# Moving the powers of C and the Toeplitz taps of a state-space group behind the chain of its states

## The chip, the cores and the metric

The kernel runs on one core of one Trainium2 chip. The metric is the device time of one execution in microseconds, as the median of several runs. The core has five engines that each work through a queue of their own in order: PE (TensorE, matrix products; its weight loads are shown as PEld), DVE (VectorE), ACT (ScalarE), POOL (GpSimd) and SP (SyncE, which here only issues DMAs). An instruction that waits holds up everything behind it in its queue.

## What is computed

One layer of a hybrid decoder, for a prompt of 1024 tokens and for 8 sequences of 4 new tokens each, D_MODEL 1024. The normed input is multiplied with one matrix whose 3072 columns are `x_ssm | z_ssm | q | k | v | z_attn`, 512 each. One branch is a state-space layer (S5), the other a dilated sliding-window attention; both are normed, joined and projected out. The change is in the state-space branch:

```python
bu_re = jnp.einsum('btgc,gpc->btgp', u, Bb_re)      # 32 groups of 16 channels, 64 complex states each
...
_, _, x_re, x_im = lax.associative_scan(_complex_affine_combine, (a_re, a_im, bu_re, bu_im), axis=1)
y = (jnp.einsum('btgp,gcp->btgc', x_re, C_re.astype(f32))
     - jnp.einsum('btgp,gcp->btgc', x_im, C_im.astype(f32))
     + D.astype(f32).reshape(N_SSM_GROUPS, SSM_GROUP) * u)
```

Each group has a diagonal complex transition `lam`; its states are driven by 16 input channels through B and read out through C.

## The kernel before

**The stage around the change.** The input projection is cut into 12 blocks of 256 columns. For each block two loads bring the weights (`load_w`, L220, on SP), eight pairs of instructions split them into a high and a low part (ACT L142 and DVE L143, `split`; both operands of L143 lie in SBUF), and PE multiplies them with the normed input, three passes each (L314 for blocks whose output is transposed, L294 for the blocks of v). ACT and DVE evict the results (L335 to L344, L378, L379), and SP stores them. Blocks 8 and 0 come first. From the seven following blocks (1, 9, 5, 2, 3, 7, 4) each is interleaved with a step of the state-space layer, which takes its 32 groups in eight sets of GO = 4, called groups below: `ssm(o)` prepares set o, `outputs(o)` reads it out.

```python
    outs = [ssm(0)]
    for o, blk in enumerate(SSM_BLOCKS):
        outs.append(ssm(o + 1))
        if o == len(SSM_BLOCKS) - 1:
            outs[o]()
        in_proj(blk)
        if o < len(SSM_BLOCKS) - 1:
            outs[o]()
    outs[-1]()
```

**What `ssm(o)` does.** Time is cut into chunks of L = 8 steps. SP loads the inputs of the set, `chunk` (L580), which blocks 0 and 1 have stored to `d_u`. Then, in the text's order:

- *B's powers*: POOL multiplies tables into `wa` and `wb` (L594, L595), DVE adds them (L596), PE turns them (L600), ACT copies them to `wt` (L601).
- *C's powers and the taps*: POOL multiplies into `f2` and `f2b` (L606, L607), DVE adds them (L608). POOL makes the diagonal of D (`di`, L611). PE multiplies B with C's powers (L615), ACT copies the result to `tap` (L618, four copies), POOL adds `di` (L619), and eight DMAs on SP (L622) lay the taps out as a Toeplitz matrix in `tpl`. `tpl` is used in turn, one of two.
- *the phases*: POOL multiplies tables into `rc`, `q0`, `rs`, `q1` (L634, L635, L637, L638), DVE combines them (L636, L639).
- *the chain of the states*: PE multiplies the inputs with `wt` (L648), DVE turns the result by the phases (L650 to L656), runs the scan over the chunks (L659), POOL turns it back into `xx` (L663 to L665) and DVE adds the halves (L666); ACT copies the last state and the start states (L667, L669).

`outputs(o)` then multiplies C's powers with the states (L678) and the Toeplitz matrix with the inputs (L679) on PE, adding both in one bank; ACT applies GELU (L681) and SP stores `yo` to `d_y` (L682).

**Buffers.** `wa`, `wb`, `f2b`, `q0`, `q1` and `tap` share four buffers (tag `gen`); `u` has three; `rc`, `rs`, `f2`, `xx` and `wt` have two each. PE's banks for L615 and for L648 are the same pair (tag `ss`).

**What sets the order.** In this stage no order is written out. The framework (`schedule_with_timeline_sim=True`, L1817) lays the instructions of each engine in a queue by a timeline of its own: where several are ready, the one that stands first in the text goes first; the buffers of a tag are handed out in the text's order too. So the text's order is a priority. Behind the stage (L740 on) the steps follow a plan that the kernel works out itself.

## Time and profile before

| | us |
|---|---|
| median of 3 runs | 705.58 (705.45 to 707.25) |
| the profiled execution | 704.87 |
| its span | 703.1 |
| PE busy in the span | 650.1 |
| DVE, ACT, POOL busy | 486.1, 318.3, 294.1 |
| mean granted clock of TensorE | 0.962 of full speed |

The times of instructions come from one profiled execution. Starts count from the start of its span. A line L143 is line 143 of the kernel before; the line is that of the call inside a helper where a helper records the instruction. A row such as `2.54 <-DVE f L608` means that the engine sat idle for 2.54 us before the instruction and that L608 on DVE ended that.

### The profile page before, as it was taken

The page shows a single profiled execution, that of the slowest core. Times are in us where ns is not written, and L with a number is a line of the kernel's source. Part 1 is how long each engine was busy: PE and PEld are TensorE (multiplying, and loading weights), DVE is VectorE, ACT ScalarE, POOL GpSimd, SP SyncE. Part 2 cuts the span into 40 slices and gives each one's busy share as a digit, 9 for nine tenths or more (in the row PEclk, how much of TensorE's full clock was granted, in tenths as well). Part 3 has the DMA queues.
Part 4 walks back from the last instruction along what each step waited for, and adds up shares of the span by engine and source line. Part 5 has one row for each costly group of instructions (what it writes and reads, how often), then busy time and mean ns, then how long its engine had stood idle before and what let it go on. Part 6 is the DMA issues. An engine that isn't in the chain of part 4 may idle for free.

```text
span 703.1 us, 12224 instructions
## 1 busy us (share of the span) xinstructions
PE 650.1 (92%) x4122; PEld 594.0 (84%) x4122; DVE 486.1 (69%) x1147; ACT 318.3 (45%) x745; POOL 294.1 (42%) x292
## 2 busy tenths in 40 slices
PE   7999896999999999959898989899999799999995
PEld 5999885999989999959888979778566599887995
DVE  4997969457797672334865787488667788965386
ACT  6762251043144252343432333277466578852363
POOL 2425687545674452004767630044233345520032
PEclk9999999899999999979999889999999799999999
DMA  8713313243432553588767744598999534028023
GB/s 278 232 32 131 116 46 112 70 153 108 125 119 71 169 173 112 209 262 235 241 200 230 235 130 152 155 285 280 309 271 296 186 110 146 18 76 281 12 98 150
DMA packets 79055, 116.22 MB, mean 165 GB/s; under 512 B 15856, under 2 KB 45424, under 8 KB 78992
## 3 DMA queue, kind: packets, MB, share of 16 engines
q1 hardware_dynamic: 78992, 115.44, 52.4%
q8 instruction: 33, 0.54, 0.3%
q14 instruction: 30, 0.25, 0.1%
HBM read 83.60 MB, written 30.62 MB: 162 GB/s over the span
## 4 chain that ended last, share of the span: by engine, by line
PE 53%; DVE 17%; DMA 12%; POOL 7%; issue 4%; ACT 4%; SPq 2%; DVEq 0%; POOLq 0%; ACTq 0%
PE mm L314 13%; PE fo L1632 5%; PE ops L1537 4%; PE mm L294 4%; DMA ct<-in_cache_v_dram 4%; PE mm L1023 4%; PE ss L294 3%; PE tp L294 3%; PE ss L1480 3%; PE tp L1522 3%; POOL dm L978 3%; DMA ct<-in_cache_k_dram 3%; DVE win L143 3%; DVE pm L1483 1%; PE fo L1348 1%
## 5 line engine op out<-in xcount | busy, mean ns | idle before, releaser
L314 PE MATMUL mm<-xT,win 128*128 128x352 f32 x1008 | 172.9, 328 | 3.7 <-DVE eq L379 1.3
L314 PEld LDWEIGHTS mm<-xT,win 128*128 128x128 f32 x1008 | 163.0, 190 | 5.1 <-DVE eq L379 1.6
L1023 PE MATMUL mm<-xT,win 128*128 128x352 f32 x432 | 78.9, 338 | 2.8 <-DVE win L1005 2.8
L1503 POOL TENSOR_SCALAR pm<-pm,rd 128x128 f32<-128x128 f32 (+3 forms) x64 | 48.5, 760 | 72.3 <-DVE rd L1499 56.9
L1023 PEld LDWEIGHTS mm<-xT,win 128*128 128x128 f32 x432 | 72.5, 197 | 3.6 <-DVE win L1005 3.4
L978 POOL TENSOR_TENSOR dm<-ct,dq 128x512 f32<-128x512 f32 x40 | 51.6, 1314 | 53.0 <-DMA ct<-in_cache_k_dram 34.1
L1495 ACT ACTIVATE pm<-pm,mn 128x128 f32<-128x128 f32 (+3 forms) x64 | 49.5, 773 | 20.2 <-DVE mn L1483 17.9
L294 PE MATMUL mm<-win,xT 128*128 128x256 f32 x384 | 53.5, 294 | 1.7 <-DVE win L143 1.5
L143 DVE SCALAR_TENSOR_TENSOR win<-wst,gin,win 128x256 fp32r<-128x256 f32 x72 | 50.0, 742 | 5.5 <-ACT win L142 5.4
L1529 DVE TENSOR_TENSOR pl<-tp,ph 128x512 fp32r<-128x512 f32 (+1 forms) x80 | 50.2, 633 | 5.1 <-ACT ph L1526 4.8
L1526 ACT ACTIVATE ph<-tp 128x512 fp32r<-128x512 f32 (+1 forms) x80 | 43.1, 547 | 22.4 <-PE tp L1522 16.4
L1632 PE MATMUL fo<-wo,gh 128*128 128x512 f32 x192 | 51.8, 412 | 0.0
L294 PEld LDWEIGHTS mm<-win,xT 128*128 128x128 f32 x384 | 49.2, 197 | 2.6 <-DVE win L143 2.1
L810 PE MATMUL gl<-yh,wg 128*128 128x272 f32 (+1 forms) x256 | 51.1, 298 | 0.0
L1483 DVE CUSTOM_DVE_ANT_0 pm<-ss,maskp 128x512 f32<-128x512 f32 (+2 forms) x64 | 37.1, 582 | 16.5 <-PE ss L1480 16.1
L1522 PE MATMUL tp<-ident,pm 128*128 128x128 f32 x288 | 45.8, 278 | 0.0
L810 PEld LDWEIGHTS gl<-yh,wg 128*128 128x128 f32 x256 | 42.5, 200 | 0.0
L1632 PEld LDWEIGHTS fo<-wo,gh 128*128 128x128 f32 x192 | 35.5, 194 | 6.9 <-DVE mn L1483 0.2
L1522 PEld LDWEIGHTS tp<-ident,pm 128*128 128x128 f32 x288 | 34.7, 142 | 7.3 <-issue 2.1
L1480 PE MATMUL ss<-ka,qt 128*128 128x512 f32 (+2 forms) x96 | 36.8, 385 | 2.3 <-DMA ka<-d_k 2.3
L981 DVE TENSOR_REDUCE scd<-dm 128x8 f32<-128x512 f32 x40 | 27.1, 682 | 17.2 <-POOL dm L978 16.9
L810 PE MATMUL gl<-yl,wg 128*128 128x272 f32 (+1 forms) x128 | 37.6, 294 | 0.0
(391 smaller groups left out, 1369.6 us busy)
## 6 DMA issues: line engine op xcount, KB each, us to landing
wst<-in_w_in_dram SPq DMA_DIRECT2D x24, 512.0 KB
ct<-in_cache_k_dram SPq DMA_DIRECT2D x48, 256.0 KB
ct<-in_cache_v_dram SPq DMA_DIRECT2D x48, 256.0 KB
xt<-in_x_prompt_dram SPq DMA_DIRECT2D x8, 512.0 KB
wst<-in_w_out_dram SPq DMA_DIRECT2D x8, 512.0 KB
xres<-in_x_prompt_dram SPq DMA_DIRECT2D x8, 512.0 KB
qt<-d_q SPq DMA_DIRECT2D x32, 128.0 KB
qw<-d_q SPq DMA_DIRECT2D x32, 128.0 KB
```

What stands on the lines that cost most here:

```text
L143: V.scalar_tensor_tensor(lo, src, scale, f(hi), op0=OP.mult, op1=OP.subtract)
L294: T.matmul(out, lhs(a, kt), w(b, kt)[:, c0:c0 + cn], start=(n == 0), stop=(n == 3 * ktn - 1))
L314: T.matmul(p, w(b, kt)[:, c * 128:c * 128 + 128], x(a, kt), start=(n == 0), stop=(n == 23))
L810: T.matmul(p, wg[:, b, kt, c:c + 128], o.y[a][:, kt, :, :o.w], start=(n == 0), stop=(n == 11))
L978: GP.tensor_tensor(out=y.m, in0=y.c, in1=x.q, op=OP.mult)
L1023: T.matmul(x.p, o.w[kt][:, b, c * 128:c * 128 + 128], xT[a][:, kt, 352 * k:352 * k + 352], start=(kt == 0 and j == 0), stop=(kt == 7 and j ...
L1480: T.matmul(x.p[c][:, :w], q[:, i % 4 * 128:i % 4 * 128 + 128], o.ka[:, 512 * c:512 * c + w], start=(m == 0), stop=(m == 1))
L1495: S.activation(x.pm[:, :n], x.pm[:, :n], AF.Exp, scale=-1.0, bias=x.mn[:, nch - 1:nch], accum_out=x.dn)
L1503: a = op(PO, 0.02 + n * 0.0012, lambda: GP.tensor_scalar(x.pm[:, :n], x.pm[:, :n], x.rd, 1.0, op0=OP.mult, op1=OP.mult), pr, [a], give=["rd"])
L1522: T.transpose(x.p[:, n * 128:n * 128 + 128], o.rows[2 * m + u].pm[:, j * 128:j * 128 + 128], ident)
L1529: V.tensor_tensor(out=x.l[:, :w], in0=x.p[:, :w], in1=f(x.h[:, :w]), op=OP.subtract)
L1632: T.matmul(o.f[hf], o.g[u][:, i, k], wo[0][:, j, 2 * u + k, hf * 512:hf * 512 + 512], start=(u + k + n == 0), stop=(u + k + n == 4))
```

## The change

The block that makes C's powers, the taps and their Toeplitz layout is moved inside `ssm(o)`: it stood between the transposed powers of B and the phases, and stands now at the end, behind the last instruction of the chain of the states. No instruction is added, taken away or changed in shape. PE's L615 now comes behind L648 in the text, POOL's L606, L607, L611 and L619 behind L663 to L668, and SP's eight L622 are the last DMAs of `ssm(o)`.

```diff
--- before.py
+++ after.py
@@ -601,27 +601,6 @@
         S.activation(wt, p, AF.Copy)
 
 
-        sh9 = [128, GO, 9, CH]
-        f2, f2b = wk(sh9, "f2"), wk(sh9, "f2b")
-        GP.tensor_tensor(out=f2, in0=pw(pr, 0, 9), in1=bc(cst, 9), op=OP.mult)
-        GP.tensor_tensor(out=f2b, in0=pw(pi, 0, 9), in1=bc(csw, 9), op=OP.mult)
-        V.tensor_tensor(out=f2, in0=f2, in1=f2b, op=OP.add)
-
-        di = wk([16, GO, 16], "di")
-        GP.tensor_tensor(out=di, in0=ident[:16, :16].unsqueeze(1).to_broadcast([16, GO, 16]),
-                         in1=dd[:, gs].unsqueeze(2).to_broadcast([16, GO, 16]), op=OP.mult)
-        p = ss_ps([128, 128])
-        for g in range(GO):
-            T.matmul(p[32 * g:32 * g + 16], bb[:, g0 + g, :], f2[:, g, 0:8, :].rearrange("p t c -> p (t c)"), start=True, stop=True)
-        tap = wk([16, GO, 128], "tap")
-        for g in range(GO):
-            S.activation(tap[:, g], p[32 * g:32 * g + 16], AF.Copy)
-        GP.tensor_tensor(out=tap[:, :, 0:16], in0=tap[:, :, 0:16], in1=di, op=OP.add)
-        tpl = tpls[o % 2]
-        for s in range(8):
-            SY.dma_start(tpl[s::8, :, 16 * s:], tap[:, :, 0:128 - 16 * s])
-
-
         shr = [128, GO, 8, 16]
         rc, rs_, q0, q1 = wk(shr, "rc"), wk(shr, "rs"), wk(shr, "q0"), wk(shr, "q1")
 
@@ -668,6 +647,27 @@
         GP.memset(xx[:, :, 0:1], 0.0)
         S.activation(xx[:, :, NC:], x0[:, gs, :], AF.Copy)
 
+
+        sh9 = [128, GO, 9, CH]
+        f2, f2b = wk(sh9, "f2"), wk(sh9, "f2b")
+        GP.tensor_tensor(out=f2, in0=pw(pr, 0, 9), in1=bc(cst, 9), op=OP.mult)
+        GP.tensor_tensor(out=f2b, in0=pw(pi, 0, 9), in1=bc(csw, 9), op=OP.mult)
+        V.tensor_tensor(out=f2, in0=f2, in1=f2b, op=OP.add)
+
+        di = wk([16, GO, 16], "di")
+        GP.tensor_tensor(out=di, in0=ident[:16, :16].unsqueeze(1).to_broadcast([16, GO, 16]),
+                         in1=dd[:, gs].unsqueeze(2).to_broadcast([16, GO, 16]), op=OP.mult)
+        p = ss_ps([128, 128])
+        for g in range(GO):
+            T.matmul(p[32 * g:32 * g + 16], bb[:, g0 + g, :], f2[:, g, 0:8, :].rearrange("p t c -> p (t c)"), start=True, stop=True)
+        tap = wk([16, GO, 128], "tap")
+        for g in range(GO):
+            S.activation(tap[:, g], p[32 * g:32 * g + 16], AF.Copy)
+        GP.tensor_tensor(out=tap[:, :, 0:16], in0=tap[:, :, 0:16], in1=di, op=OP.add)
+        tpl = tpls[o % 2]
+        for s in range(8):
+            SY.dma_start(tpl[s::8, :, 16 * s:], tap[:, :, 0:128 - 16 * s])
+
         return lambda: outputs(o, f2, xx, tpl, chunk)
 
     def outputs(o, f2, xx, tpl, chunk):
```

## Rows read from the trace of the kernel before

**Rows 1.** The page: busy us, share and instructions of each engine.

```profile
PE 650.1 (92%) x4122; PEld 594.0 (84%) x4122; DVE 486.1 (69%) x1147; ACT 318.3 (45%) x745; POOL 294.1 (42%) x292
```

**Rows 2.** Windows: busy us (instructions) of PE, PEld, DVE, ACT, POOL; clock; DMA.

```profile
60.00:80.00 20.00, 17.46 (x107) 16.99 (x106) 16.05 (x12) 7.26 (x18) 18.00 (x19) 0.91 0.18 60
...
100.00:120.00 20.00, 13.96 (x99) 12.94 (x99) 19.85 (x26) 6.24 (x14) 17.53 (x15) 1.00 0.25 74
...
180.00:200.00 20.00, 20.00 (x138) 19.75 (x138) 15.76 (x27) 7.18 (x22) 11.71 (x13) 1.00 0.20 54
```

**Rows 3.** Windows of 2 us, the same columns: the two drops of the clock.

```profile
76.00:78.00 2.00, 2.00 (x8) 2.00 (x8) 2.00 (x3) 0.20 (x1) 2.00 (x2) 0.50 0.02 4
...
124.00:126.00 2.00, 2.00 (x11) 2.00 (x11) 1.64 (x4) 0.00 (x0) 1.40 (x3) 0.50 0.53 148
```

**Rows 4.** Waits of PE, 55 to 290 us: total us, times, longest.

```profile
PE ss L615 <- DVE f L608: 5.2, 2, 2.6
PE tp L600 <- DVE wa L596: 1.9, 1, 1.9
```

**Rows 5.** Timeline of PE: start, us, what, count, idle before and its releaser.

```profile
74.60 0.41 PE L615 MATMUL ss<-f,bb 128*16 128x128 f32 x8 [2.54 <-DVE f L608]
74.94 5.66 PE L314 MATMUL mm<-xT,win 128*128 128x352 f32 x24
...
120.75 0.63 PE L615 MATMUL ss<-f,bb 128*16 128x128 f32 x8 [2.65 <-DVE f L608]
...
143.81 4.10 PE L314 MATMUL mm<-xT,win 128*128 128x352 f32 x24
...
275.01 0.39 PE L678 MATMUL so<-xx,f 128*128 128x136 f32 x2
```

**Rows 6.** Timeline of DVE, same columns, in the two stretches.

```profile
67.08 7.47 DVE L608 TENSOR_TENSOR f<-f,f2b 128x576 f32<-128x576 f32 x1 [1.11 <-POOL f2b L607]
74.47 6.47 DVE L143 SCALAR_TENSOR_TENSOR win<-wst,gin,win 128x256 fp32r<-128x256 f32 x8
...
107.52 11.85 DVE L143 SCALAR_TENSOR_TENSOR win<-wst,gin,win 128x256 fp32r<-128x256 f32 x8
...
119.95 0.75 DVE L608 TENSOR_TENSOR f<-f,f2b 128x576 f32<-128x576 f32 x1
```

**Rows 7.** The split L143, 104 to 122 us: least, median, most ns.

```profile
L143 DVE SCALAR_TENSOR_TENSOR win<-wst,gin,win x8: 1454/1550/1630, 107.5 to 117.8; 128x256 fp32r<-128x256 f32 x8
```

**Rows 8.** The split L143 in 140 to 146 us, the same columns.

```profile
L143 DVE SCALAR_TENSOR_TENSOR win<-wst,gin,win x8: 480/483/486, 141.9 to 145.1; 128x256 fp32r<-128x256 f32 x8
```

**Rows 9.** Timeline of POOL: a pause, and the order inside one group.

```profile
84.63 0.12 POOL L324 MEMSET stp<- 128x32 f32 x1 [5.57 <-DMA d_u<-stp]
...
148.85 1.23 POOL L606 TENSOR_TENSOR f<-pr,cst 128x576 f32<-128x576 f32 x1 [9.60 <-PE so L678]
...
150.07 1.41 POOL L635 TENSOR_TENSOR q<-sink 128x512 f32<-128x512 f32 x1
...
155.77 0.62 POOL L619 TENSOR_TENSOR tap<-tap,di 16x64 f32<-16x64 f32 x1 [1.26 <-ACT tap L618]
```

**Rows 10.** Groups by line, 60 to 240 us: count, busy, mean ns, idle.

```profile
L608 DVE TENSOR_TENSOR f<-f,f2b 128x576 f32<-128x576 f32 x7 | 15.7, 2239 | 7.6 <-POOL xx L668 6.5 <-POOL f2b L607 1.1
...
L618 ACT ACTIVATE tap<-ss 16x128 f32<-16x128 f32 x28 | 7.5, 268 | 6.7 <-PE ss L615 5.0 <-POOL wa L594 1.4
```

**Rows 11.** Waits of SP's queue, 55 to 300 us.

```profile
SPq L220 <- DVE win L143: 43.1, 8, 14.9
SPq L622 <- POOL tap L619: 15.5, 4, 10.4
```

**Rows 12.** The moved tap DMAs, all eight groups: first and last start.

```profile
L622 SPq DMA_DIRECT2D tpl<-tap x64: 542/593/1631, 85.0 to 264.7; - x64
```

**Rows 13.** Timeline of SP's queue at the end of the stage.

```profile
285.22 1.93 SPq L682 DMA_DIRECT2D d_y<-yo  x3
```

**Rows 14.** Timeline of PE behind the stage.

```profile
309.01 0.40 PE L1085 MATMUL tp<-ident,pdT 128*32 128x128 f32 x1 [7.48 <-ACT pdT L1034]
```

## The prediction

> **What bounds the kernel now.** I read the page first: PE is busy for 92% of the span [rows 1]. An average hides stages, so the windows of 20 us over the state-space stage (about 60 to 285 us) come next. From 128 us on PE has no room: 20.00 of 20 us at full clock in the window shown, with DVE at 15.8 and POOL at 11.7. The room lies before: 17.46 of 20 us from 60, 13.96 of 20 from 100 [rows 2]. Moving instructions can only pay in those two holes, or behind the stage. The waits of PE name what ends the idle time: 5.2 us in two waits for L608, the add that makes the powers of C, and 1.9 us in one for L596 [rows 4]. PE takes its queue in order, so the four small tap products of L615 hold up the projection behind them. The timeline gives the places, 2.54 us up to 74.60 and 2.65 us up to 120.75 [rows 5]. After each hole the granted clock is 0.50, the lower of its two levels (1.2 GHz of 2.4) [rows 3]; so 24 projection matmuls that take 4.10 us at full clock took 5.66 us behind the first one [rows 5].
>
> The timeline of DVE shows why L608 is late. In the first hole one L608 lasts 7.47 us, where the one at 119.95 lasts 0.75; the eight splits of the next block's weights (L143) stand behind it and end at 80.94. In the second hole the splits themselves are slow: 11.85 us for eight [rows 6]. The split takes 1454 to 1630 ns there and 480 to 486 ns in a stretch where POOL stands idle, up to 148.85 [rows 7 to 9]. So DVE instructions with two operands in SBUF pay for POOL's work beside them, and PE waits for those two: splits and L608.
>
> The Trainium skill, page "SBUF — State Buffer", section "Who interferes with whom", says that a DVE instruction with two SBUF inputs and a GpSimd instruction that reads SBUF exclude each other, and that the later one waits until the first has finished. By that the first L608 would pay at most one POOL instruction, some 1.4 + 0.75 = 2.2 us as an estimate; the trace has 7.47, over five times L635's 1.41 [rows 6, 9], so the measured row decides, and the splits' 1.55 us do agree with the rule.
>
> **The change part by part.** Nothing is added or removed; per group the block of C's powers and taps goes behind the chain. It issues on POOL L606 (1.23 us), L607 (of its shape, taken alike), L611 and L619 (0.62 us; L611 of its shape, taken alike), 3.7 us [rows 9]; on DVE L608, 2.24 us in the mean, 0.75 alone [rows 6, 10]; four ACT copies L618 at 0.27 us [rows 10]; on PE the products L615, 0.41 us [rows 5]; on SP eight DMAs L622 at a median of 0.593 us, 4.7 us of queue [rows 12]. The order on each engine isn't the text's: the framework takes, of what it thinks ready, the earliest in the text. So the move changes priorities, and by the ring of four buffers that wa, wb, f2b, tap, q0 and q1 share, it changes gates. Now q0 and q1, which the chain's phases need, are asked for behind f2b and tap. The rows of a middle group show it: POOL idles 9.60 us for L606, which waits for the output products L678 of two groups before, and only then comes L635, which reads nothing but tables made at the start [rows 9]. After the change q0 and q1 follow wa and wb, and the chain no longer waits for the powers' buffer of its own group; wa of the next group stands behind tap instead.
>
> *First hole.* L608 and L615 no longer stand before the splits; L636 and L639 do. What is late next is the splits. They must follow block 0's last matmuls and the ACT halves, which begin at about the time of L608, so they can start some 5 us before 74.47. Bounds: at best the whole 2.54 us of idle and the 5.66 − 4.10 = 1.56 us of clock return, −4.1. At worst POOL, whose q products are now free to run without a pause, makes ten DVE instructions (eight splits, L636, L639) pay 1.55 us each: 15.5 us from about 68.5 (an estimate: 67.08, where L608 starts today, and one POOL instruction of 1.41 us [rows 6, 9]) ends at 84.0, where the splits ended at 80.94: +3.1. In the middle of 0.48 and 1.55 us, 1.0 each, they end at 78.6, 2.3 us sooner. That hole has both kinds of split in the trace (6.47 us for eight is 0.81 each [rows 6]), so I take the middle, rounded down: −2.
>
> *Second hole.* The splits end at 107.52 + 11.85 = 119.37 and PE stays idle till 120.75, since L615 waits for the L608 that ends at 120.70 [rows 5, 6]. These 1.4 us go if L615 stands behind the projection: −1.4. Bounds: −1.4 − 2.65 − 1.9 (L600's wait, if the chain that stands before L596 is done sooner) = −6.0; and none, 0, if other rows of the chain take L608's place. The price of the splits themselves I leave as it is.
>
> *Elsewhere under PE.* From 128 to 285 us L615 and L608 lie under a PE that is full [rows 2]; taken at 0. If that cover is gone, each group pays L615's wait, about 2.6 us as in the two holes [rows 5].
>
> *SP's queue.* The DMAs of L622 move behind loads and stores of the same group: L220 (weight loads, which wait for the splits up to 14.9 us), the stores of yo, the loads of u. Now it is L622 that holds SP for up to 10.4 us till L619 [rows 11]. Weight loads behind it may come sooner; the tap tiles may come later. Their cover is the time from the last L622 of the last group, 264.7, to its first output product, 275.01 [rows 5, 12]: 10.3 us. Taken at 0; beyond the cover each us costs one on PE, where the stage ends with those products.
>
> *End of the stage.* Chain and taps of the last group can be ready earlier, and then more of its output products go into the gaps between projection chunks. Three stores L682 that run 285.22 to 287.15 [rows 13] stand ahead of the next stage's loads; those loads lead to PE's idle time of 7.48 us up to 309.01 [rows 14]. Bounds: −1.9 (all three before) and, if the taps hold the products back, +1.9. I take half of the gain, −1.
>
> Sum: −2 − 1.4 − 1 = −4.4 us. The profiled execution took 704.87 us (span 703.1 and 1.8 around it); with the change 700.5. The median of the runs is 0.7 above that execution, so the forecast is 705.58 − 4.4 = 701.2. Its own range, by half of the ends: 698 to 703.4.
>
> **The rivals.** *Both holes close.* With the chain ahead, the splits find POOL in a pause, and the clock does not fall: the first hole gives 4.1, the second 6.0, the end 1.9: −12 → 693.6. For it: each hole ends with L608 [rows 4]. Against: in the second hole eight splits took 1.55 us each while L608 was not on DVE at all [rows 6, 7].
>
> *Nothing measurable.* The moved rows are fillers; the framework puts them into the same pauses, the splits stay the last thing PE waits for, and the rest of the stage is full anyway: 705.6, with ±2. That is also the case where the order hardly changes and the change does not do what it says. For it: L608 is ready early in both texts, and POOL has pauses to fill [rows 9]. Against: the gate on q0 is a buffer, not a pause.
>
> *Slower: the chain runs too far ahead.* Its place is the second hole. Freed from the powers' buffer, the chain of one more group gets in front of the splits of block 9, because the text puts the next group before the next projection: L596, L636, L639 and L656, four DVE instructions with two SBUF operands, at 1.55 us [rows 7] 6.2 us more before PE gets its weights: 711.8. It decides from the point at which POOL no longer pauses between 62 and 107 us; today it pauses 5.57 us at 79 [rows 9] for a store of u. For it: DVE is already 19.85 of 20 us busy in that window [rows 2]. Against: the chain then goes before PE asks for the splits. The skill's rule named above is on the side of this rival, as it charges each overlap of the two engines.
>
> **How the numbers follow.** 0.3% of 705.6 is 2.1 us, about what a measurement of this kernel can tell from no change. Chances: forecast (698 to 703.4) 0.33; both holes close (below 698) 0.15; nothing (703.5 to 707.7) 0.22; slower 0.30. Faster 0.48, same 0.22, slower 0.30: the likeliest sign is faster, by little. For 8 in 10 the range must reach well into both outer cases: their prices are 693.6 and 711.8, and leaving out a tenth at each end puts it at 694.5 to 711.5. The forecast's own range is 698 to 703.4.
>
> **What would show it.** Right: L615 gone from the waits of PE before 128 us; the splits of block 1 ending before 80; L635 before L606 on POOL in each group; PE over 15.5 of 20 us from 100 to 120 and the clock at 0.50 for a shorter time; the last L678 before 284. Wrong: the splits of block 9 beginning after 107.5 with L636 and L656 of a third group in front of them; an L608 of many us holding another split; output products waiting for the tap DMAs; or PE's holes simply elsewhere, with L600 or L648 in L615's place.

## The result, and the profile after

The changed kernel takes 708.41 us in the median of 20 runs (703.64 to 712.62), the kernel before 705.27 beside it: a ratio of 1.0058, 95% interval 1.0037 to 1.0079. The ratio leaves out one slow execution of the kernel before (870.87 us), so it is not the quotient of the two medians. By it the move makes the kernel about 4 us slower; the forecast was 4.4 us faster. The profiled execution took 708.31 us.

In the changed kernel the same instructions have these lines: phases L613, L614, L616, L617 (POOL) and L615, L618 (DVE); chain L627 to L648 with `xx` added in L645 (DVE); moved block L653, L654 (POOL), L655 (DVE add, was L608), L658 (POOL, `di`, was L611), L662 (PE, was L615), L665 (ACT), L666 (POOL, diagonal added to the taps, was L619), L669 (SP, was L622).

The page and four windows of the changed kernel, with the columns of [rows 1] and [rows 2]:

```profile
PE 647.8 (92%) x4122; PEld 594.6 (84%) x4122; DVE 499.8 (71%) x1147; ACT 319.8 (45%) x745; POOL 294.6 (42%) x292
```

```profile
60.00:80.00 20.00, 17.19 (x106) 16.88 (x106) 15.83 (x14) 6.65 (x16) 16.55 (x17) 0.98 0.19 62
100.00:120.00 20.00, 17.75 (x133) 17.03 (x133) 17.36 (x27) 8.25 (x19) 12.34 (x12) 0.91 0.44 128
140.00:160.00 20.00, 16.63 (x105) 15.80 (x105) 16.81 (x28) 5.88 (x18) 10.51 (x11) 0.91 0.32 83
220.00:240.00 20.00, 17.24 (x115) 16.98 (x114) 16.89 (x23) 7.53 (x19) 9.48 (x10) 1.00 0.53 148
```

The work is the same, 1147 instructions on DVE, but DVE is busy 13.7 us longer than in [rows 1]. In the windows, 100 to 120 us gained what was hoped for: PE 17.75 us where [rows 2] has 13.96. The loss is where the prediction wrote nothing: in the kernel before PE had 20.00 us in both of the last two windows, 146 and 138 matmuls; now 16.63 and 17.24 us, 105 and 115 matmuls, and the first of the two at a granted clock of 0.91 in the mean. These two windows of the kernel before:

```profile
140.00:160.00 20.00, 20.00 (x146) 19.57 (x145) 10.77 (x20) 8.15 (x23) 8.79 (x9) 1.00 0.47 145
220.00:240.00 20.00, 20.00 (x138) 19.59 (x137) 11.26 (x17) 9.16 (x25) 9.34 (x9) 1.00 0.52 157
```

The waits of PE from 55 to 290 us, in the form of [rows 4]:

```profile
PE mm L314 <- DVE win L143: 6.2, 2, 3.4
PE mm L314 <- DVE stp L344: 4.2, 2, 2.8
PE ss L662 <- DVE f L655: 1.9, 1, 1.9
PE ss L662 <- DVE nst L632: 1.8, 1, 1.8
PE mm L314 <- ACT ek L384: 1.6, 1, 1.6
```

The taps' wait for the add fell from 5.2 us in two to 1.9 in one. In its place PE waits 6.2 us for splits of weights (L143) and 4.2 us for DVE's evictions (L344). The timelines of DVE and POOL show why DVE is late. In what follows a small product is one of POOL's two products on 16 partitions, `di` and the tap add, and POOL's train is a run of its instructions without a pause. First the wait of 3.37 us, with DVE, POOL and PE one below the other (start, duration, what, count):

```profile
140.57 1.88 DVE L615 TENSOR_TENSOR rc<-rc,q 128x512 f32<-128x512 f32 x1
142.38 6.00 DVE L143 SCALAR_TENSOR_TENSOR win<-wst,gin,win 128x256 fp32r<-128x256 f32 x5
```

```profile
141.87 0.76 POOL L666 TENSOR_TENSOR tap<-tap,di 16x64 f32<-16x64 f32 x1
142.60 1.39 POOL L616 TENSOR_TENSOR rs<-cosk,sink 128x512 f32<-128x512 f32 x1
143.96 1.35 POOL L617 TENSOR_TENSOR q<-sink,cosk 128x512 f32<-128x512 f32 x1
145.28 1.21 POOL L654 TENSOR_TENSOR f2b<-pi,csw 128x576 f32<-128x576 f32 x1
146.45 0.46 POOL L658 TENSOR_TENSOR di<-ident,dd 16x64 f32<-16x64 f32 x1
```

```profile
146.82 3.00 PE L314 MATMUL mm<-xT,win 128*128 128x352 f32 x11 [3.37 <-DVE win L143]
```

One of these splits alone lasts 4.38 us, where a split takes 0.48 undisturbed [rows 8] (the splits from 140 to 150 us: least, median, most ns):

```profile
L143 DVE SCALAR_TENSOR_TENSOR win<-wst,gin,win x8: 464/472/4384, 142.4 to 149.4; 128x256 fp32r<-128x256 f32 x8
```

It is the first of the five. It begins inside L666, a product on 16 partitions, and ends inside L658, the next one on 16 partitions; the three POOL instructions between them run one after another at their usual 1.2 to 1.4 us. The longest such row, from 116 to 128 us:

```profile
118.38 7.40 DVE L645 SCALAR_TENSOR_TENSOR xx<-zz,sg,xx 128x512 f32<-128x512 f32 x1 [2.51 <-POOL zz L644]
```

```profile
118.42 0.31 POOL L666 TENSOR_TENSOR tap<-tap,di 16x64 f32<-16x64 f32 x1
118.67 0.09 POOL L647 MEMSET xx<- 128x4 f32 x1
118.73 1.23 POOL L653 TENSOR_TENSOR f<-pr,cst 128x576 f32<-128x576 f32 x1
119.93 1.39 POOL L617 TENSOR_TENSOR q<-sink,cosk 128x512 f32<-128x512 f32 x1
121.28 1.21 POOL L654 TENSOR_TENSOR f2b<-pi,csw 128x576 f32<-128x576 f32 x1
122.47 1.39 POOL L613 TENSOR_TENSOR rc<-cosk 128x512 f32<-128x512 f32 x1
123.82 1.40 POOL L616 TENSOR_TENSOR rs<-cosk,sink 128x512 f32<-128x512 f32 x1
125.19 0.73 POOL L658 TENSOR_TENSOR di<-ident,dd 16x64 f32<-16x64 f32 x1
```

From 60 to 290 us there are seven DVE rows over 2.3 us, all with two operands in SBUF: 5.72 us at 72.56, 3.43 at 96.86, 7.40, 4.38, 3.14 at 167.90, 6.18 at 190.49, 4.86 at 222.01. Four begin inside a product on 16 partitions, two 0.04 us before one, one 0.14 us behind one. Six end inside the next `di`, and that at 72.56 ends at 78.28, when POOL's train has ended at 78.00. Not every such meeting makes a long row: at 251.58 an L615 begins inside L666 and lasts 0.80 us, and it is POOL's next product that takes 1.88 us.

The kernel before has one row over 2.3 us, the L608 of 7.47 us [rows 6]; another, L656 at 103.32, has 2.30 us and ends inside a `di` too. What stood beside L608 was to be seen in the old trace too:

```profile
67.00 0.28 POOL L611 TENSOR_TENSOR di<-ident,dd 16x64 f32<-16x64 f32 x1
67.25 1.40 POOL L634 TENSOR_TENSOR rc<-cosk 128x512 f32<-128x512 f32 x1
...
74.01 1.79 POOL L635 TENSOR_TENSOR q<-sink 128x512 f32<-128x512 f32 x1
```

L608 begins at 67.08, inside that `di`. It ends at 74.55 while POOL is at work: its train runs on to 79.07, no small product stands there, and only L635 beside the end takes 1.79 us instead of 1.41 [rows 9]. What ended this row is open. Most of the other fifteen small products of the kernel before meet a pause, or a DVE row that takes an operand from PE's bank or ends soon.

At the end of the stage the first matmul of the next one (L1023) begins at 290.56 us instead of 284.79. The gap of [rows 14] is unchanged, 7.53 us.

### The profile page after: what moved, and what is told of

It is laid out like the page before. It is cut to its first block, busy times and chain, and to the rows that moved or that the text cites. A ratio compares the mean times of both kernels' runs of the same rounds, so it can differ in the third digit from the quotient of the medians.

```text
span 706.5 us, 12217 instructions
## 1 busy us (share of the span) xinstructions
PE 647.8 (92%) x4122; PEld 594.6 (84%) x4122; DVE 499.8 (71%) x1147; ACT 319.8 (45%) x745; POOL 294.6 (42%) x292
## 4 chain that ended last, share of the span: by engine, by line
PE 49%; DVE 18%; DMA 12%; POOL 8%; issue 7%; SPq 3%; ACT 3%; DVEq 0%; POOLq 0%; ACTq 0%
PE mm L314 13%; PE fo L1632 5%; PE ops L1537 5%; PE ss L294 3%; PE tp L294 3%; PE ss L1480 3%; PE tp L1522 3%; PE mm L1023 3%; POOL dm L978 3%; DMA ct<-in_cache_k_dram 2%; DVE win L143 2%; PE mm L294 2%; DMA wst<-in_w_in_dram 2%; PE fo L1348 2%; DMA ct<-in_cache_v_dram 2%
## 5 line engine op out<-in xcount | busy, mean ns | idle before, releaser
L314 PE MATMUL mm<-xT,win 128*128 128x352 f32 x1008 | 172.8, 328 | 11.9 <-DVE win L143 6.2
L314 PEld LDWEIGHTS mm<-xT,win 128*128 128x128 f32 x1008 | 162.9, 190 | 14.2 <-DVE win L143 6.8
L1023 PE MATMUL mm<-xT,win 128*128 128x352 f32 x432 | 79.1, 338 | 2.3 <-DVE win L1005 2.2
L1023 PEld LDWEIGHTS mm<-xT,win 128*128 128x128 f32 x432 | 72.7, 198 | 3.3 <-DVE win L1005 3.1
L294 PE MATMUL mm<-win,xT 128*128 128x256 f32 x384 | 53.4, 294 | 0.4 <-DVE win L143 0.4
L1632 PE MATMUL fo<-wo,gh 128*128 128x512 f32 x192 | 53.7, 424 | 0.0
L143 DVE SCALAR_TENSOR_TENSOR win<-wst,gin,win 128x256 fp32r<-128x256 f32 x72 | 47.8, 705 | 3.4 <-ACT win L142 3.3
L294 PEld LDWEIGHTS mm<-win,xT 128*128 128x128 f32 x384 | 49.3, 198 | 1.0 <-DVE win L143 0.6
L810 PE MATMUL gl<-yh,wg 128*128 128x272 f32 (+1 forms) x256 | 49.6, 293 | 0.0
L810 PEld LDWEIGHTS gl<-yh,wg 128*128 128x128 f32 x256 | 41.2, 194 | 0.0
L645 DVE SCALAR_TENSOR_TENSOR xx<-zz,sg,xx 128x512 f32<-128x512 f32 x8 | 22.4, 2795 | 23.8 <-POOL zz L644 23.8
```

The lines of the kernel that those rows point to most:

```text
L143: V.scalar_tensor_tensor(lo, src, scale, f(hi), op0=OP.mult, op1=OP.subtract)
L294: T.matmul(out, lhs(a, kt), w(b, kt)[:, c0:c0 + cn], start=(n == 0), stop=(n == 3 * ktn - 1))
L314: T.matmul(p, w(b, kt)[:, c * 128:c * 128 + 128], x(a, kt), start=(n == 0), stop=(n == 23))
L810: T.matmul(p, wg[:, b, kt, c:c + 128], o.y[a][:, kt, :, :o.w], start=(n == 0), stop=(n == 11))
L1023: T.matmul(x.p, o.w[kt][:, b, c * 128:c * 128 + 128], xT[a][:, kt, 352 * k:352 * k + 352], start=(kt == 0 and j == 0), stop=(kt == 7 and j ...
L1632: T.matmul(o.f[hf], o.g[u][:, i, k], wo[0][:, j, 2 * u + k, hf * 512:hf * 512 + 512], start=(u + k + n == 0), stop=(u + k + n == 4))
```

## The experiments

The names are those of the expectations. Theory B: a DVE instruction with two operands in SBUF that meets a POOL product on 16 partitions stands still until POOL's train pauses or the next such product comes; the move brings more of these meetings. Theory A: without pauses POOL's longer train costs by itself, whatever its shapes. The rival of order: the move's loss is one of order (taps, gates, queue), and the long rows are a sign of it. Ratios are to the kernel before, timed on the same chip, with 95% intervals. A long row is a DVE row over 2.3 us.

**The small products on DVE.** In both kernels the two POOL products on 16 partitions are given to DVE:

```diff
-        GP.tensor_tensor(out=di, in0=ident[:16, :16].unsqueeze(1).to_broadcast([16, GO, 16]),
+        V.tensor_tensor(out=di, in0=ident[:16, :16].unsqueeze(1).to_broadcast([16, GO, 16]),
...
-        GP.tensor_tensor(out=tap[:, :, 0:16], in0=tap[:, :, 0:16], in1=di, op=OP.add)
+        V.tensor_tensor(out=tap[:, :, 0:16], in0=tap[:, :, 0:16], in1=di, op=OP.add)
```

The changed kernel so edited:

> The kernel after, with the two small products on 16 partitions (the diagonal of D and its addition to the taps) on DVE in place of POOL. Theory A (POOL's work now stands in one long train behind the chain, and DVE instructions with two SBUF operands, and what is queued behind them, wait in it): the train keeps its eight large products, so PE's waits for splits and evictions between 140 and 262 us stay at 6 us or more, time 707 to 709. Theory B (only where a small 16-partition product runs just as a DVE instruction comes does DVE wait for the whole train): the two 6 to 7 us rows of the chain's last addition shrink to 2 us or less, PE's wait of 1.4 us at 198 us goes, time 705 to 707. Rival (the loss comes from the order of PE's and SP's queues, not from POOL beside DVE): 708, rows as they are.

The kernel before so edited:

> The kernel before, with the same two small products on DVE. POOL's order is otherwise the old one. Theory B: the 7.47 us row of the addition of C's powers at 67 us shrinks to about 2 us, the eight splits behind it come up to 5 us sooner, PE's idle time of 2.54 us goes with most of the half clock behind it: 701 to 703. Theory A without B: that row stays at 5 us or more and the time within 2 us of 705.

Measured: 700.93 us, ratio 0.9940 (0.9911 to 0.9968), and 702.52, 0.9977 (0.9942 to 1.0012). Neither has a DVE row over 2.3 us. The changed kernel's time lies below what any of the theories gave. The changed kernel gains 1.2% by it, the one before 0.2%, within its uncertainty. Small products on DVE come at other times than on POOL, so the orders differ too; later pairs hold them still.

**Only the taps behind the chain**, the powers of C in front as before. The instructions that make `f2` stay where they stood, and from here on the block is moved:

```diff
         V.tensor_tensor(out=f2, in0=f2, in1=f2b, op=OP.add)
-        di = wk([16, GO, 16], "di")
...
+        di = wk([16, GO, 16], "di")
```

> Half of the change: C's powers (two POOL products and their addition) stay in front of the phases, and only the taps (diagonal, tap products, copies, addition, eight DMAs) go behind the chain. Theory A: POOL still meets the powers' buffer, and its wait for the output products, ahead of the phases, so the train behind the chain is cut in two as before; PE waits between 140 and 262 us stay under 4 us, time 704 to 706.5. Rival (order of PE's tap products and of the eight DMAs on SP): they are placed as in the kernel after, so the loss of 3 us is here too, 707 to 709.

Measured: 709.63, 1.0055 (1.0024 to 1.0085), the loss of the whole change, with three long rows (5.83, 7.57 and 6.09 us), each beginning inside or just before a small product. So the taps, which hold both small products, are enough. The time is the one expected of the rival of order, not of theory A; this run does not part that rival from theory B.

**The kernel before with an open ring**: `f2b` and `tap` get buffers of their own, so nothing of theirs waits for the ring of four.

```diff
-            if name in ("wa", "wb", "f2b", "q0", "q1", "tap"):
+            if name in ("wa", "wb", "q0", "q1"):
```

> The text order of before, but the second product of C's powers and the taps get buffers of their own, so that the phases' products no longer queue for a buffer behind the taps. Theory A (what slows is that the gate in front of the phases falls, not the text's order): POOL's pause in front of the powers no longer holds the phases, the train behind the chain grows to 12 us or more as in the kernel after, time 707 to 710. Rival (order of the tap block itself): 704 to 706, as before.

Measured: 711.79, 1.0102 (1.0066 to 1.0139). The L608 of [rows 6] grew:

```profile
66.98 11.32 DVE L608 TENSOR_TENSOR f<-f,f2b 128x576 f32<-128x576 f32 x1 [1.13 <-POOL f2b L607]
```

Behind the `di` at 66.91 POOL runs without a pause till 77.69, eight products and three fills, and L608 ends at 78.30. A second long row begins without a small product beside it:

```profile
100.61 5.90 DVE L596 TENSOR_TENSOR wa<-wa,wb 128x512 f32<-128x512 f32 x1 [0.94 <-POOL wb L595]
```

The last `di` ended 1.20 us earlier, at 99.41; L596 begins inside a product on 128 partitions of the same train and ends inside the next tap add. So a small product ahead in the train is enough, and DVE need not meet it. POOL's train as a whole did not become longer: from 62 to 280 us POOL has 33 pauses over 0.1 us, against 26 in the kernel before. The same with the small products on DVE:

> The kernel before with buffers of their own for the second product of C's powers and for the taps, and the two small products on DVE. Theory A (the gate in front of the phases, once gone, costs by the long train alone): still 707 or more. Theory B (the gate's fall is harmless, the small products made the loss): 700 to 704, no DVE row over 2.3 us.

Measured: 715.63, 1.0153 (1.0103 to 1.0204), without a long row. Theory B expected the loss to go; it did not. The time is the one expected of theory A, but POOL has 24 pauses here, about as many as the kernel before, so the train's length is not shown to be the cause. PE waits 5.8 us for one eviction (L338), 3.9 for L379, 3.9 for splits and 3.2 for L413. An open ring in the old order costs by itself, by a way that stays open, and B is not the only way to lose time in this stage.

**One shape alone.** Three runs of the changed kernel with the tap add on DVE and `di` on POOL, with 16 partitions and 64 elements, 128 partitions and 64, 16 partitions and 512. The first two have the same order in every queue; in the second `di` multiplies another table. `di` of the second is therefore not D's diagonal, and that kernel does not compute the layer; it serves for its time. The edits of the second and the third:

```diff
-        di = wk([16, GO, 16], "di")
-        GP.tensor_tensor(out=di, in0=ident[:16, :16].unsqueeze(1).to_broadcast([16, GO, 16]),
-                         in1=dd[:, gs].unsqueeze(2).to_broadcast([16, GO, 16]), op=OP.mult)
+        di = wk([128, GO, 16], "di")
+        GP.tensor_tensor(out=di, in0=ident[:, :16].unsqueeze(1).to_broadcast([128, GO, 16]),
+                         in1=mag[:, gs].unsqueeze(2).to_broadcast([128, GO, 16]), op=OP.mult)
...
+        di = wk([16, GO, 128], "di")
+        GP.tensor_tensor(out=di, in0=ident[:16, :].unsqueeze(1).to_broadcast([16, GO, 128]),
+                         in1=dd[:, gs].unsqueeze(2).to_broadcast([16, GO, 128]), op=OP.mult)
```

> The kernel after with the addition to the taps on DVE; the diagonal product on 16 partitions and 64 elements stays on POOL. Theory B (a small POOL product on 16 partitions that meets a DVE instruction with two SBUF operands leaves DVE waiting until the next such product, a pause or a fill): long DVE rows of 3 us or more come back, one to four of them, each begun while the diagonal product runs; time 702 to 706, between the two kernels. If the diagonal is harmless and only the tap addition does it: no row over 2.3 us, 701.

> The same, but the diagonal product on all 128 partitions, 64 elements each (with another table as its second operand, so that the diagonal is not that of D). If the number of partitions makes the long rows: none over 2.3 us, time 700 to 702.5. If the shortness of the product makes them: as with 16 partitions.

> The same, but the diagonal product on 16 partitions with 512 elements each, as long as the others (about 1.3 us). If the number of partitions makes the long rows: they are there, one to four, begun while this product runs, time 703 to 707. If its shortness does: none over 2.3 us.

Measured: 713.25 (1.0110, 1.0078 to 1.0143) with 16 partitions, **702.36** (0.9968, 0.9934 to 1.0001) with 128, 718.2 (1.0172, 1.0134 to 1.0211) with 16 and eight times the length. The long rows: seven splits and phase adds, none, eight. For 16 partitions theory B had expected fewer rows (one to four) and less time (702 to 706 and 703 to 707 us). The same place in the first two, DVE, the splits' least, median and most, and POOL; with 16 partitions:

```profile
69.06 9.45 DVE L143 SCALAR_TENSOR_TENSOR win<-wst,gin,win 128x256 fp32r<-128x256 f32 x5
78.43 0.68 DVE L618 TENSOR_TENSOR rs<-rs,q 128x512 f32<-128x512 f32 x1
```

```profile
L143 DVE SCALAR_TENSOR_TENSOR win<-wst,gin,win x8: 471/472/5720, 69.1 to 79.8; 128x256 fp32r<-128x256 f32 x8
```

```profile
71.76 0.47 POOL L658 TENSOR_TENSOR di<-ident,dd 16x64 f32<-16x64 f32 x1
72.19 1.41 POOL L613 TENSOR_TENSOR rc<-cosk 128x512 f32<-128x512 f32 x1
73.56 1.41 POOL L616 TENSOR_TENSOR rs<-cosk,sink 128x512 f32<-128x512 f32 x1
```

with 128 partitions:

```profile
69.36 6.56 DVE L143 SCALAR_TENSOR_TENSOR win<-wst,gin,win 128x256 fp32r<-128x256 f32 x5
75.84 1.71 DVE L618 TENSOR_TENSOR rs<-rs,q 128x512 f32<-128x512 f32 x1
```

```profile
L143 DVE SCALAR_TENSOR_TENSOR win<-wst,gin,win x8: 471/1446/1643, 69.4 to 79.2; 128x256 fp32r<-128x256 f32 x8
```

```profile
72.05 0.48 POOL L658 TENSOR_TENSOR di<-ident,mags 128x64 f32<-128x64 f32 x1
72.48 1.61 POOL L613 TENSOR_TENSOR rc<-cosk 128x512 f32<-128x512 f32 x1
74.04 1.60 POOL L616 TENSOR_TENSOR rs<-cosk,sink 128x512 f32<-128x512 f32 x1
```

`di` lasts the same, 0.47 and 0.48 us. Behind 128 partitions the engines take turns, DVE at some 1.45 us a split and POOL at 1.60 a product; behind 16 POOL runs at 1.41 and one split stands for 5.72 us. It is the number of partitions, not the length and not the order. The other table of the second kernel is not the reason either: two whole kernels below take D itself on 128 partitions and have no long row.

Two of the fifteen rows begin 1.4 us behind the end of `di`, beside products on 128 partitions of its train, so here too DVE need not meet the small product itself. With 16 partitions and 64 elements:

```profile
118.17 0.81 POOL L658 TENSOR_TENSOR di<-ident,dd 16x64 f32<-16x64 f32 x1
118.95 1.40 POOL L617 TENSOR_TENSOR q<-sink,cosk 128x512 f32<-128x512 f32 x1
```

```profile
120.39 4.41 DVE L618 TENSOR_TENSOR rs<-rs,q 128x512 f32<-128x512 f32 x1 [1.55 <-POOL q L617]
```

All fifteen end 0.3 to 0.6 us behind the end of POOL's train; no second small product stands in it that could end them sooner.

**No table products at all.** The eight table products on POOL are replaced by two fills each, which read nothing, as here and in the three other pairs:

```diff
-        GP.tensor_tensor(out=rc, in0=ea(ear), in1=eb(ebr), op=OP.mult)
-        GP.tensor_tensor(out=q0, in0=ea(eai), in1=eb(ebi), op=OP.mult)
+        GP.memset(rc, 0.01), GP.memset(rc, 0.02)
+        GP.memset(q0, 0.01), GP.memset(q0, 0.02)
```

> The kernel after, with the eight products that POOL makes from tables (B's powers, C's powers, phases) each replaced by two fills of the same tile, which write and read nothing: the state-space branch is not computed from its tables. Theory A and B alike: POOL is about as busy in the stage, but DVE's rows with two operands fall to 0.5 to 0.8 us except beside the three chain products; PE's waits between 60 and 290 us fall under 4 us, and the stage ends 8 us or more sooner than in the kernel after, time 696 to 701. Rival (queue order of PE and SP): the waits stay, 707.

Measured: 688.74, 0.9783 (0.9723 to 0.9843), less than the 696 to 701 expected. No long row, though both small products are still on POOL: five times an L615 begins inside a `di` with fills behind it, and lasts 0.78 us. So the small product alone does not make a long row; in every long row of these runs products that read stand behind it. By an estimate from their rows, the DVE instructions with two operands take 1 to 3 us together over what they take alone, against some 56 in the changed kernel and some 43 in the kernel before. The stage then ends at 267.19 us. So the eight table products cost the changed kernel some 20 us, and the long rows are only a part of that. Another part may be POOL's shorter work: two fills take 1.03 to 1.15 us where one of the products takes 1.25 to 1.53 in the mean.

**The changed kernel again, and the diagonal added on PE.** In the second D's diagonal is made once on DVE and added by 64 small PE products in the taps' bank; POOL has no small product left.

```diff
+    dia = sw.tile([16, G, 16], F32, name="dia")
+    V.tensor_tensor(out=dia, in0=ident[:16, :16].unsqueeze(1).to_broadcast([16, G, 16]),
+                    in1=dd.unsqueeze(2).to_broadcast([16, G, 16]), op=OP.mult)
...
+            T.matmul(p[32 * g:32 * g + 16, 0:16], ident[:16, :16], dia[:, g0 + g, :], start=False, stop=True)
...
-        GP.tensor_tensor(out=tap[:, :, 0:16], in0=tap[:, :, 0:16], in1=di, op=OP.add)
```

> The kernel after, unaltered, beside the two others of this call on the same chip: 707 to 710, a ratio of 1.004 to 1.008 to before; in its trace at least five DVE rows over 3 us, each begun beside a POOL product on 16 partitions.

> The kernel after without any small product on POOL: the diagonals of D are made once, by DVE, ahead of the groups, and PE adds them to the tap products in the same bank (four products of 16x16 per group), so that the addition on 16 partitions goes too. Theory B: no DVE row over 2.3 us, time 699 to 702, as with both on DVE or 1 us better. If something other than the small products made the loss: 706 or more.

Measured: 708.14, 1.0054 (1.0021 to 1.0087), with the same seven long rows; and 706.27, 1.0028 (0.9995 to 1.0061), with none. Theory B expected 699 to 702 of the second; 706 or more was to speak for another cause. PE's waits of the second are about 5 us, and PE's busy time from 60 to 290 us is 224.8 us against 213.9, of which the added products are 6.8. That these took what the rows gave back is likely, not shown. By the intervals it is not clearly better than either kernel.

**Both kernels, the small products on 128 partitions, every queue in the same order.** `di` as above, and the second product writes 128 partitions of the taps' first columns, from `di` alone. So D and the tap products of these columns are left out, and the two kernels serve for their times:

```diff
-        tap = wk([16, GO, 128], "tap")
+        tap = wk([128, GO, 128], "tap")
...
-        GP.tensor_tensor(out=tap[:, :, 0:16], in0=tap[:, :, 0:16], in1=di, op=OP.add)
+        GP.tensor_tensor(out=tap[:, :, 0:16], in0=di, in1=di, op=OP.add)
```

> The kernel after with every queue in the same order, instruction for instruction; only the two small products of POOL run on 128 partitions in place of 16, 64 elements each, on other operands (the diagonal is not that of D, and its addition leaves the tap products out). Theory B (the small products' 16 partitions make DVE wait for POOL's whole train, and that is what the change costs): no DVE row over 2.3 us, PE's waits for splits and evictions between 140 and 262 us gone, time 699 to 703. Rival (the new order of the queues costs by itself, the long rows only go with it): 706 or more.

> The same for the kernel before, its queues unaltered. Theory B: the one long DVE row of 7.47 us goes, time 701 to 704, and the distance to the changed kernel with 128 partitions is what the text's move does without the long rows: between 3 us less and 1 us more. Rival: 705, and that distance is +3 us as between the two kernels themselves.

Measured: the changed kernel **695.79**, 0.9885 (0.9843 to 0.9927), less than the 699 to 703 expected; the kernel before **701.1**, 0.9968 (0.9942 to 0.9994). No long row in either. With the intervals added as if independent, the 16 partitions cost the changed kernel 1.0058 − 0.9885 = 1.7 ± 0.5%, 12.2 ± 3.3 us, and the kernel before 0.3 ± 0.3%, 2.3 ± 1.8 us. The rival of order fails here: with the same order the loss is gone.

The traces show where. From the first matmul of block 5 to the first of the next stage (L1023) the kernel before takes 141.0 us and the changed one 149.4; with 128 partitions it is 141.3 and 142.0.

By the ratios the move without the small shape is even a gain: 0.9885 − 0.9968 = −0.8 ± 0.5%, −5.9 ± 3.5 us. The two profiled executions show hardly any of it in the stage: it ends at 278.91 us in the new order and at 279.08 in the old one, a later product (L810) first begins at 306.22 and 306.95, and the spans are 696.2 and 698.4. So the smaller end is the safer reading, and where a gain would lie is not shown. The windows of the changed kernel with 128 partitions:

```profile
60.00:80.00 20.00, 20.00 (x130) 19.98 (x129) 15.84 (x17) 6.70 (x16) 17.53 (x18) 1.00 0.36 116
100.00:120.00 20.00, 17.00 (x141) 15.98 (x140) 16.34 (x27) 6.23 (x17) 12.41 (x11) 1.00 0.44 129
140.00:160.00 20.00, 18.35 (x122) 17.28 (x123) 14.40 (x28) 4.07 (x15) 13.62 (x12) 1.00 0.48 146
220.00:240.00 20.00, 19.82 (x136) 19.14 (x135) 15.18 (x29) 6.88 (x23) 9.77 (x10) 1.00 0.64 191
```

and of the kernel before with 128:

```profile
60.00:80.00 20.00, 20.00 (x134) 19.60 (x133) 15.15 (x14) 7.31 (x20) 19.09 (x21) 1.00 0.36 116
100.00:120.00 20.00, 15.74 (x116) 14.51 (x115) 19.31 (x22) 6.25 (x18) 16.96 (x15) 0.95 0.37 108
```

The first hole is gone from its window in both, with the clock at 1.00: the 60 to 80 us window of [rows 2] was short because of the small products, wherever L608 stood in the text. A part of it only moved on: from 80 to 100 us PE has 17.43 us in the old order and 17.96 in the new, where the kernels themselves have 19.44 and 20.00; over the 40 us it runs 245 and 247 matmuls instead of 237 and 232. The second hole is the move's own: 15.74 us of PE in the old order, 17.00 in the new. But in the window from 140 to 160 us, where the new order has 18.35, the old one has 20.00.

**Whole kernels without the small shape.** Four versions that compute everything, all in the new text order. The first two keep both POOL products, on 128 partitions with D padded by zeros: in the first ACT copies the diagonal over the taps' first columns so that all partitions hold something, in the second the taps have two fixed buffers filled once; in the third D's diagonal is made once on DVE and added there, eight small DVE instructions; in the fourth DVE adds D's diagonal where the taps leave PE's bank, four small instructions per group. The lines that each brings, in that order:

```diff
+        S.activation(tap[:, :, 0:16], di, AF.Copy)
...
+        tap = taps[o % 2]
...
+        V.tensor_tensor(out=tap[:, :, 0:16], in0=tap[:, :, 0:16], in1=dia[:, gs], op=OP.add)
...
+            V.scalar_tensor_tensor(out=tap[:, g, 0:16], in0=ident[:16, :16], scalar=dd[:, g0 + g:g0 + g + 1], in1=p[32 * g:32 * g + 16, 0:16],
+                                   op0=OP.mult, op1=OP.add)
```

> A whole kernel with the change and without the long rows: the table of D lies on 128 partitions, zero beyond the sixteenth, the diagonal and its addition to the taps run on 128 partitions on POOL, and one more ACT copy (128x64) fills the rest of the taps' buffer first. If the order of the queues stays near that of the kernel after: no DVE row over 2.3 us, 695 to 700. If the additional copy alters the order: still no such row, 699 to 705.

> The same, but the taps have two fixed buffers that are filled once, in place of one of the four shared ones and the additional copy; that also takes the taps out of the ring of buffers. No DVE row over 2.3 us. If the open ring does no harm: 695 to 700; if it does, as in the kernel before with buffers of its own for the taps, 705 or more.

> The changed kernel with D's diagonal made once for all groups on DVE and added to the taps on DVE; POOL has no product on 16 partitions left, and DVE eight small instructions more per pass instead of the sixteen of the kernel with both products on DVE (700.93 us). Theory (the rest of that kernel's distance to the two products on 128 partitions, 700.93 against 695.79, is the price of the small instructions in DVE's queue, of which half go): 697 to 700 us, no DVE row over 2.3 us. Rival (the distance is the changed order of POOL's train, which loses its pauses for the small products): 701 to 706, like the kernel that added the diagonal on PE (706.27), and PE's waits of 55 to 298 us no shorter than 15 us.

> The changed kernel with the diagonal of D added by DVE where the taps leave PE's bank: four DVE instructions per group on 16 partitions and 16 columns with one operand in PE's bank, in place of both POOL products; ACT copies the other 112 columns. Theory (long DVE rows need a product of POOL on 16 partitions): no DVE row over 2.3 us and not slower than before: 696 to 702. Rival (a DVE instruction on 16 partitions does the same to POOL's train, or the four waits for PE's tap products block DVE): over 704, with waits of PE for the splits or the chain behind these instructions.

Measured: 708.79 (1.0057, 1.0028 to 1.0085), 703.88 (0.9996, 0.9973 to 1.0020), 702.98 (0.9974, 0.9942 to 1.0005) and 705.81 (1.0028, 0.9999 to 1.0057). No DVE row over 2.3 us in any, so few partitions on DVE do not do what few on POOL do. Yet none reaches 695.79, and all are slower than theory B expected (702 us at most for three of them, 705 for the first). In each the order of the queues differs from that of the changed kernel: in the first, PE waits 4.0 us for one eviction of outputs and 3.0 for the chain, and the window from 100 to 120 us has a mean clock of 0.76; in the second the splits of block 9 cost PE 5.4 us; the third has the waits of the kernel with both products on DVE, nearly one for one, so the number of small DVE instructions is not their cause; the fourth ends the stage earlier than the kernel before but takes longer behind it in its profile. What keeps these from 695.79 stays open. The whole kernel with the lowest median is the changed one with both small products on DVE, 700.93 us, the only one of them whose interval lies below the kernel before.

## Why the prediction was wrong

*What bounds the stage*: right. DVE instructions with two SBUF operands pay for POOL's work, and PE waits for those.

*First hole, −2*: did not come. The splits end at 80.87 us instead of 80.94; L615's idle time of 2.54 us became 2.81 us of L314 waiting for a split:

```profile
78.34 1.68 PE L314 MATMUL mm<-xT,win 128*128 128x352 f32 x7 [2.81 <-DVE win L143]
```

The working took each row beside POOL at 0.5 to 1.55 us and moved the 7.47 us of L608 away with L608. But that price belonged to the DVE instruction that came upon `di` and the train behind it, not to L608. Now a split does, for 5.72 us. With 128 partitions the window was full wherever L608 stood.

*Second hole, −1.4, bound −6.0*: right in sign and place, and too small. The first matmul of block 9 (L294) begins at 103.44 us instead of 108.07, −4.6. Its splits start at 100.91 instead of 107.52, and five of the eight take 0.47 us instead of some 1.55: their price is the part that the step had left as it was.

*Elsewhere under PE, taken at 0*: **the step that failed.** The cover was read from PE's 20.00 of 20 us in one window [rows 2], though from 200 to 220 us PE had 18.84; and the step priced only what it would cost if L615's wait came back, 2.6 us a group. It did not ask what the moved POOL instructions do to the DVE instructions beside which they come to stand. The cost was not in the moved DVE add, 0.95 us in the mean now, but in L143, L615 and L645. PE, full before, lost 3.37 us of its 20.00 from 140 to 160 and 2.76 from 220 to 240. From the first matmul of block 5 to the next stage it took 149.4 us instead of 141.0: +8.5 where the sum had 0. With 128 partitions these were 142.0 and 141.3, so nearly all of it hangs on the small shape.

*SP's queue, taken at 0*: right. SP waits 15.7 us for the tap add, 5.9 at most, and no output product waited for the tap DMAs.

*End of the stage, −1*: it came out at +5.8: block 5 begins 2.7 us sooner (141.12 instead of 143.81), what the second hole left, and the loss above is added. The rest behind the stage gave 2.4 us back (the span is 3.4 us longer).

*Order on POOL*: right. The phases no longer wait for the ring behind the powers, and POOL's train has fewer pauses, 17 over 0.1 us from 62 to 280 us instead of 26. Fewer pauses alone were not dear, once the shape was taken away.

*The rivals*: slower had 0.30 and 711.8 us, near the 708.41 that came, but by another mechanism: its place was the second hole, which gained, and its point, POOL's pause at 79 us, was not what decided. No rival priced a DVE row of several microseconds per group, though one stood in [rows 6]. The range held the time only because it had been drawn wide for other reasons. The forecast's own range, 698 to 703.4, does not follow from its ends: these add up to −12.0 and +5.0, and half of the way to them from −4.4 gives 697.4 to 705.9.

*The Trainium skill*, page "SBUF — State Buffer", section "Who interferes with whom", lets the later of the two engines wait until the first has finished. By that no DVE row here would pay more than one POOL instruction. With 128 partitions the traces agree: the splits shown reach 1.643 us, beside POOL products of 1.60, and no two-operand DVE row in the stage is over 2.02. With 16 they do not: one DVE row stood over six products and a fill (7.40 us), another lasted 11.32. The prediction had seen the contradiction, said that the measured row decides, and then priced with rows of the other kind.

## What to carry to other kernels

A row that lasts over three times what its rule allows (7.47 us against 2.2) is a mechanism that has not been understood: find what stands beside it before moving work past it, for the price stays with the neighbour and not with the row. When POOL's order changes, list for each of its instructions which DVE rows with two SBUF operands it will meet; cover on PE protects only as long as those finish. Keep POOL products on 16 partitions out of a train that such rows will meet. Both ways round them took the long rows away in every run, but of the whole kernels only the one with both products on DVE gained; of the two that spread them over 128 partitions none did.

## What was not expected of the hardware

In POOL's train a product on 16 partitions, mostly of 0.3 to 0.8 us, let a DVE instruction with two SBUF operands that began beside it, or up to 1.4 us behind it, stand for 3.1 to 11.3 us: mostly over the rest of POOL's train, or until the next such product. With fills behind the small product it did not (0.78 us). The same product on 128 partitions, in the same order of all queues, let the engines take turns (1.45 and 1.60 us each), and the kernel took 702.36 us instead of 713.25. Why the number of partitions decides, why not every meeting does it, and whether other numbers than 16 and 128 do the same, no run here shows.
